# Mixing's steps, priorities, retention and layer-end squares rearranged in a two-layer hybrid trunk

## The chip, the core and the metric

The kernel runs on one core of a Trainium2 chip. The core has TensorE (PE: matmuls, with weight loads shown as PEld), VectorE (DVE), ScalarE (ACT), GpSimd (POOL) and SyncE (SP, which here only issues DMAs). Each takes its instructions in the order in which they were queued at build time, and waits on semaphores for what it needs from the others. The metric is the device time of one execution in microseconds (us), lower is better.

## The reference

The program is a decoder trunk of two layers over 512 tokens of width 1024. Each layer does this (cut to what matters):

```
h = rmsnorm(x, g_mix)
(cq, ckv, kr, aq, ak, av, qi, ki, wi, rq, rk, rv, rg) = split(h @ w_in)
# A) latent attention, 8 heads
q  = rmsnorm(cq) @ w_uq;  kv = rmsnorm(ckv) @ w_ukv
o_a = softmax(causal((q_nope.k_nope + rope(q_rope).rope(kr)) * scale)) @ v
# B) DSA: index scores choose 128 keys per query, 4 heads share one key/value head
score = sum over 8 index heads of wi * relu(rope(qi).rope(ki)), causal
sel = top_k(score, 128);  o_b = softmax over sel of (rope(aq).rope(ak) * scale) @ av
# C) retention, 4 heads: scores times gamma^(i-j), causal, no softmax
ret = (decay * (rope(rq).rope(rk) / 8)) @ rv;  o_c = silu(rg) * groupnorm(ret)
x = x + concat(o_a, o_b, o_c) @ w_out
x = x + square(relu(rmsnorm(x, g_mlp) @ w_ff1)) @ w_ff2
```

After the second layer comes one more rmsnorm.

## The kernel before

Activations lie transposed, features on the 128 partitions and 512 tokens in the free dimension, in tiles of 128x512. Nearly every product is done in reduced-precision F32 (`FR`), with each operand split in a high and a low part: `split` (line 236) copies the high part on ScalarE and forms the remainder on VectorE, `mm3` (148) adds three matmuls. Weights come by DMA from SP's queue and are split the same way (`wsplit`, 203), the remainder on VectorE or GpSimd. A plain F32 matmul, as `pv_step` (335) uses it for MLA's values with a single term, is one call but shows as two matmul instructions in the trace.

A layer has two parts. *Mixing* is a list of steps in the string `ORDER`, read at the end of the layer loop. `qi` are the index queries, `tk` the token-major tiles (`token_tiles`: values of DSA and retention, index weights), `ix` the index scores of one block of 128 queries (ScalarE's relu, VectorE's weighted sum), `rq`/`rk` retention's queries and keys, `rg` its gate, `aq` DSA's queries, `kv`/`cq` the compressed inputs with `kvf`/`cqf` their norms (`LowRank.factor`), `mk`, `k`, `q`, `v`, `rr` MLA's keys, queries, values and rotary parts by pair or round, `m` the maxima of a pair of heads, `a` the attention of one head, `dm` the maxima of DSA, `d` DSA's attention for one query block, and `F` flushes the delayed value products. Two kinds of work are dealt out between them: `tN` takes N steps of top-k from a list of 51 (16 rounds for each of three query blocks, each a MAX8 and a MATCH_REPLACE8 on VectorE at lines 761 and 762, then three masks at line 766), and `rN` takes N of 16 retention scores. A number beyond the list's end does nothing. `dm` needs all three masks.

What the engines do is laid out at build time. The program is traced in the order of the steps; `hp(key)` (line 80) lets the instructions inside it stand `PRI[key]` places further ahead (a negative number: further behind); a planner takes the ready instruction that stands first, engine by engine, by its own estimate of times, and the queues that come out are fixed. Only keys that an `hp` call names act: `w` weights, `e` evacuations of products, `t` top-k, `q`, `qm`, `v`, `k`, `rr`, `pv`, `done`, `ret`, `st` statistics, `tab` tables, `cq`, `dm`, `rg`, `aq`, `rope`.

Retention's value product: `ret_score` forms scores of one key block in PSUM, splits them in high and low tiles, GpSimd multiplies both with a causal mask, and two reduced matmuls with lhsT holding the high and low values of one head give a 128-row result whose halves `ret_done` adds.

The *MLP* part is 32 up-projections and a seven-product (Strassen-like) down-projection (`mlp`, from 424). While its last products run, the next layer's norm begins: `half_squares` (363) squares and adds x for half the columns, `half_stats` (370) reduces the partitions with matmuls by a column of ones, in F32, and `half_bcast` spreads the result. The early half (columns 256 to 511) is done inside the last weight loop, the late half after it.

Of the kernel before, what the change touches and what calls it, by code (L numbers as in the profile page):

```python
# [10 lines left out]
F32 = mybir.dt.float32  # L11
# [6 lines left out]
P = 128  # L18
# [32 lines left out]
OPT_R = 0  # L51
MHI = 'aaap'
MLO = 'vp'
ORDER = 'qi0 rg0 qi1 tk ix1 ix2 F rq0 ix3 rk0 rq1 r1 t2 r1 r1 t3 rk1 t4 rg1 aq1 r1 r1 aq0 F t2 t2 F F F F F t2 F F kv0 kv1 F F t1 F F r2 cq0 t2 t2 r1 r1 cq1 r4 kvf kvc t2 cq2 cq3 t5 r7 cq4 t1 t4 r16 t4 t2 cq5 r12 F F r6 r12 t1 F r2 v0 r16 r14 F r14 r9 cqf r2 t4 mk F t2 r1 r2 cqc r2 r2 r3 F t1 r11 rr0 t1 t4 t4 q0 r4 k1 t5 F k0 t2 r4 F t2 r2 q1 t4 r6 t4 r2 F t10 t10 t3 t4 m0 r2 r6 t2 r5 m1 r3 r2 r1 t3 t2 t5 a0 a1 t2 k2 t4 t4 dm t7 t4 r10 r1 t9 rr1 r1 t7 t3 r2 t4 a2 q2 a3 q3 t3 r3 m2 r7 t6 r10 r2 d2 t5 d3 d0 t15 d1 k3 t4 t2 r2 t2 t1 t3 m3 v1 a4 t8 t1 a6 F t3 r2 t4 t59 t2 r1 t6 r2 a7 r2 t3 t1 t3 a5 t2 t3 F r1 F r3 r2 r10 F r2 F'
PRI = {'fin': 0, 'w': 99, 'e': 59, 't': -225, 'rope': 0, 'split': 133, 'q': -16, 'qm': 0, 'rr': 0, 'v': 5, 'k': 0, 'att': 0, 'pv': 0, 'done': -70, 'ret': -44, 'st': 65, 'x': 0, 'tab': -20, 'cq': 0, 'tok': 15, 'idx': 0, 'dm': 8, 'rg': 0, 'km': 0, 'qi': 0, 'aq': 0}
TOPK = 128
NEG = -1e30
GONE = -3e38
# [10 lines left out]
def trunk_kernel(ctx, tc, xT, gains, win, wtk, wuq, wukv, wout, wff1, wff2, tabs, cf, cb, outT):  # L69
# [20 lines left out]
    def g_(dt=F32, shape=None):  # L90
        return S("g", GB, shape, dt)
# [21 lines left out]
    def p_():  # L113
        return S("p", PB, [P, 2, T], FR)

    def v_(shape, dt=FR):
        return S("v", 2, shape, dt)
# [21 lines left out]
    def R(ap):  # L139
        return ap.bitcast(F32)  # L140

    def tt(eng, op, out, a, b):
        (nc.vector if eng == "v" else nc.gpsimd).tensor_tensor(out, a, b, op=op)
# [92 lines left out]
    def split(src, hi, lo, eng="a"):  # L236
        copy_fr(hi, src, eng)
        nc.vector.tensor_sub(lo, src, R(hi))
# [87 lines left out]
    def push(f):  # L326
        pend.append(f)
        while len(pend) > LAG:
            pend.popleft()()
# [33 lines left out]
    def half_squares(xv, n, cols):  # L363
        t = [g_(F32, [P, 2, 256]) for _ in range(2)]
        for i in range(2):
            nc.scalar.activation(t[i], xv[2 * n + i][:, :, cols], AF.Square)
        nc.vector.tensor_add(t[0], t[0], t[1])
        return t[0]

    def half_stats(sums):  # L370
        with hp("st"):
            ps = sc_ps()
            for n, s in enumerate(sums):
                for m in range(2):
                    for b in range(2):
                        nc.tensor.matmul(ps[:, b : b + 1], s[:, m, b * P : (b + 1) * P], ones,  # L376
                                         start=n + m + b == 0, stop=n + m == 2, skip_group_check=True)
            return rstd(ps[:, :2], 1024)

    def half_bcast(y, ps):  # L380
# [43 lines left out]
    def mlp(l, xv, u, rb, nxt):  # L424
# [172 lines left out]
        for j in range(4, 8):  # L597
            w4[j] = weights(j, "a22", in_qk)
            if j == 5:
                for q in range(4):  # L600
                    for m in range(2):
                        nxt.tile(xv, q, m, early)
                nxt.finish(xv, early, [half_squares(xv, n, early) for n in range(2)])
            if j < 6:
                for n in range(2):
                    mul(p4, w4[j][n], operand(2 * j + n, 1), 2 * j + n)
        sums = []
        for m in range(4):
            for i in range(12, 16):
                mul(p4, w4[i // 2][i % 2], operand(i, 1), i, ms=(m,))  # L610
            with hp("e"):
                o = [xv[m // 2 * 2 + blk][:, m % 2, late] for blk in range(2)]
                nc.vector.tensor_add(o[0], o[0], p4[m][0])
                nc.vector.tensor_sub(o[1], o[1], p4[m][0])
            for blk in range(2):
                nxt.tile(xv, m // 2 * 2 + blk, m % 2, late)
            if m % 2:
                sums.append(half_squares(xv, m // 2, late))
        return sums

    xsrc = xT
    for l in range(DEPTH):
# [79 lines left out]
        wtoks = []  # L702

        def token_tiles():
            vall = v_([P, 4 * T])
            vd = S("vd", 1, [P, NB, 192])
            vr = vall.rearrange("p (b h s d) -> p b h s d", b=NB, h=4, s=2)
            vt.extend((vd, None, vall.rearrange("p (b h d) -> p b h d", b=NB, h=4)))
            for c0 in (0, 128):
                nc.gpsimd.memset(vd[:, :, c0 : c0 + 64], 1.0)  # L710
            wtok = tiny(32, "wtok", 1)
            wtoks.append(wtok)
            tps = [mm_ps(), mm_ps(), o_ps(), o_ps()]
            for c in range(3):
                nk = min(3, KD - 3 * c)
                for j, (h_, l_) in enumerate(wchunk(wtk[l, c][:, : nk * 328], nk * 328, nk)):
                    k = 3 * c + j
                    ah, al = u[k]
                    for b in range(NB):
                        bs = slice(b * P, (b + 1) * P)  # L720
                        mm3(tps[b][:, :328], ah[:, bs], al[:, bs], h_, l_, k == 0, k == KD - 1)
            for b in range(NB):
                o = tps[b]
                z = g_()
                with hp("e"):
                    nc.scalar.activation(z[:, :328], o[:, :328], AF.Copy, scale=rtok[:, b : b + 1])
                nc.vector.tensor_scalar(wtok[:, b * 8 : b * 8 + 8], z[:, 320:328], IDX_SCALE, None, op0=ALU.mult)
                mu = tiny(4)
                zv = z[:, 64:320].rearrange("p (h d) -> p h d", h=4)
                nc.vector.tensor_reduce(mu, zv, axis=AX.X, op=ALU.add)  # L730
                nc.vector.tensor_scalar(mu, mu, 1.0 / 64, None, op0=ALU.mult)
                nc.vector.tensor_sub(zv, zv, mu.rearrange("p (h o) -> p h o", o=1).to_broadcast([P, 4, 64]))
                nc.scalar.activation(vd[:, b, 64:128], z[:, :64], AF.Copy)
                split(zv, vr[:, b, :, 0], vr[:, b, :, 1])

        mix = [(None, None)] * 8
        fill_top, fill_ret = deque(), deque()
# [64 lines left out]
        def ret_score(pr, e, i):  # L802
            (rq, rql), (rk, _) = rqk[3, pr], rqk[5, pr]
            q0 = P * min(i, 2)
            n = T - q0
            ps = sc_ps()[:, :n]
            ks = slice(i * P, (i + 1) * P)
            mm(ps, rk[:, e, ks], rq[:, e, q0:], True, False)
            mm(ps, rk[:, e, ks], rql[:, e, q0:], False, True)
            pt = p_()[:, :, :n]  # L810
            ph, pl = pt[:, 0], pt[:, 1]
            split(ps, ph, pl)
            w = P if i < 3 else 2 * P
            mb = m01[:, 2 * P - w :].rearrange("p (o n) -> p o n", o=1).to_broadcast([P, 2, w])
            tt(E_MSK, ALU.mult, pt[:, :, :w], R(pt[:, :, :w]), mb)
            v = vt[2][:, i, 2 * pr + e]
            push(lambda: pv_step("r", i, [(v, ph), (v, pl)], lambda o: ret_done(pr, e, o)))

        def ret_done(pr, e, o):
            with hp("ret"):  # L820
                rows = slice(64 * e, 64 * e + 64)
                if e == 0:
                    rts[pr] = g_()
                rt = rts[pr]
                half = g_()
                nc.scalar.activation(half[rows], o[64 - 64 * e : 128 - 64 * e], AF.Copy)
                nc.vector.tensor_add(rt[rows], o[rows], half[rows])
                if e == 0:
                    return
                sg = sgs[pr]  # L830
                sq = g_()
                nc.scalar.activation(sq, rt, AF.Square)
                ps = sc_ps()
                mm(ps, blk, sq, True, True)
                yv = g_()
                nc.scalar.activation(yv, ps, AF.Ln, bias=epst)
                nc.scalar.activation(yv, yv, AF.Exp, scale=-0.5)
                nc.gpsimd.tensor_mul(sq, yv, yv)
                nc.vector.scalar_tensor_tensor(sq, ps, EPS, sq, op0=ALU.add, op1=ALU.mult)
                nc.gpsimd.tensor_scalar(sq, sq, -0.5, 1.5, op0=ALU.mult, op1=ALU.add)  # L840
                nc.gpsimd.tensor_mul(yv, yv, sq)
                nc.vector.scalar_tensor_tensor(rt, rt, gcol(G0 + G_RET + pr), yv, op0=ALU.mult, op1=ALU.mult)
                nc.gpsimd.tensor_mul(rt, rt, sg)
                mh, ml = u2()
                split(rt, mh, ml)
                mix[6 + pr] = (mh, ml)
# [513 lines left out]
```

## Time and profile before

| | us |
|---|---|
| median of 3 runs | 1358.52 (1355.89 to 1358.78) |
| the profiled execution, its own time | 1358.57 |
| its span, first to last instruction | 1356.8 |
| TensorE busy | 1298.3 |
| VectorE busy | 1025.6 |
| ScalarE busy | 627.5 |
| GpSimd busy | 272.5 |

A busy TensorE is not one at its peak, because matmuls overlap and their ends are modelled. Layer 0's mixing takes about the first 350 us, its MLP ends near 685 us; layer 1 follows in the same pattern. Line numbers in the rows are those of the kernel before; a line such as 146, 238 or 143 is a helper's, so the names out<-in tell the step.

### The profile page before, as it was taken

The page shows a single profiled execution, that of the slowest core. Times are in us where ns is not written, and L with a number is a line of the kernel's source. Part 1 is how long each engine was busy: PE and PEld are TensorE (multiplying, and loading weights), DVE is VectorE, ACT ScalarE, POOL GpSimd, SP SyncE. Part 2 cuts the span into 40 slices and gives each one's busy share as a digit, 9 for nine tenths or more (in the row PEclk, how much of TensorE's full clock was granted, in tenths as well). Part 3 has the DMA queues.
Part 4 walks back from the last instruction along what each step waited for, and adds up shares of the span by engine and source line. Part 5 has one row for each costly group of instructions (what it writes and reads, how often), then busy time and mean ns, then how long its engine had stood idle before and what let it go on. Part 6 is the DMA issues. An engine that isn't in the chain of part 4 may idle for free. (4 is left out here: it accounts for less than half of the span.)

```text
span 1356.8 us, 19944 instructions
## 1 busy us (share of the span) xinstructions
PE 1298.3 (96%) x7274; PEld 1097.0 (81%) x7276; DVE 1025.6 (76%) x1728; ACT 627.5 (46%) x1083; POOL 272.5 (20%) x265
## 2 busy tenths in 40 slices
PE   9987979999999999999999898899999999999997
PEld 7866866768888888899987677666778888889997
DVE  5799997655777776797668999965558767778875
ACT  4533544654444444465536244446444444445552
POOL 3446752104000000000033467410230000000000
PEclk9989999999999999999999999999999999999998
DMA  6666422223554555466456681232235554554652
GB/s 217 175 179 183 125 73 85 92 63 109 166 176 157 184 186 172 140 209 213 153 163 175 171 206 55 78 114 75 66 109 177 192 175 156 186 184 157 198 184 72
DMA packets 82178, 201.73 MB, mean 149 GB/s; under 512 B 10240, under 2 KB 19168, under 8 KB 82080
## 3 DMA queue, kind: packets, MB, share of 16 engines
q1 hardware_dynamic: 80928, 199.41, 48.0%
q8 instruction: 57, 0.93, 0.3%
q10 hardware_dynamic: 1152, 1.05, 0.2%
q14 instruction: 41, 0.34, 0.1%
HBM read 155.68 MB, written 20.97 MB: 130 GB/s over the span
## 5 line engine op out<-in xcount | busy, mean ns | idle before, releaser
L146 PE MATMUL mm<-u,wh 128*128 128x512 f32 (+1 forms) x1776 | 552.3, 391 | 0.9 <-ACT wh L192 0.9
L146 PEld LDWEIGHTS mm<-u,wh 128*128 128x128 f32 x1776 | 332.1, 190 | 66.5 <-ACT wh L192 1.1
L146 PE MATMUL mm<-u,wl 128*128 128x512 f32 (+1 forms) x888 | 345.6, 389 | 5.7 <-DVE wl L215 5.6
L192 ACT ACTIVATE wh<-wr 128x512 fp32r<-128x512 f32 (+2 forms) x247 | 149.8, 610 | 298.7 <-PE mm L146 187.9
L215 DVE TENSOR_TENSOR wl<-wr,wh 128x512 fp32r<-128x512 f32 (+2 forms) x208 | 148.6, 716 | 85.4 <-ACT wh L192 84.2
L217 POOL TENSOR_TENSOR wl<-wr,wh 128x512 fp32r<-128x512 f32 (+2 forms) x80 | 104.6, 1308 | 487.4 <-ACT wh L192 454.8
L146 PEld LDWEIGHTS mm<-u,wl 128*128 128x128 f32 x888 | 168.3, 190 | 40.7 <-DVE wl L215 7.2
L503 DVE TENSOR_TENSOR u<-wr,u 128x1024 fp32r<-128x1024 f32 x54 | 65.9, 1224 | 25.9 <-ACT u L502 25.8
L502 ACT ACTIVATE u<-wr 128x1024 fp32r<-128x1024 f32 x54 | 57.1, 1058 | 54.3 <-PE o L516 14.1
L445 DVE TENSOR_TENSOR sm<-wr 128x512 f32<-128x512 f32 x64 | 44.2, 691 | 47.8 <-DMA wr<-in_wff 47.8
L516 PEld LDWEIGHTS sc<-g,v 128*128 128x128 f32 x576 | 72.2, 189 | 2.3
L516 PE MATMUL sc<-g,v 128*128 128x256 f32 x576 | 73.1, 281 | 0.0
L433 DVE SCALAR_TENSOR_TENSOR g<-mm,g 128x512 f32<-128x512 f32 x64 | 43.9, 686 | 15.5 <-PE mm L146 15.5
L194 POOL TENSOR_SCALAR wh<-wr 128x512 fp32r<-128x512 f32 (+3 forms) x41 | 30.5, 743 | 107.3 <-PE mm L146 54.1
L762 DVE MATCH_REPLACE8 g<-m,g 128x384 f32<-128x384 f32 (+2 forms) x96 | 51.4, 540 | 0.0
L146 PE MATMUL sc<-u,qk 97*128 97x512 f32 (+5 forms) x192 | 50.0, 384 | 0.9 <-DMA u<-mr 0.9
L516 PE MATMUL o<-g,v 128*128 128x256 f32 x384 | 50.5, 281 | 0.0
L761 DVE MAX8 m<-g 128x8 f32<-128x256 f32 (+2 forms) x96 | 49.9, 546 | 0.1
L449 ACT ACTIVATE v<-wr 128x1024 fp32r<-128x1024 f32 x32 | 34.0, 1062 | 33.2 <-DVE wr L447 33.1
L516 PEld LDWEIGHTS o<-g,v 128*128 128x128 f32 x384 | 47.5, 189 | 0.0
L516 PE MATMUL sc<-wh,u 128*128 128x256 f32 x224 | 46.1, 285 | 0.9 <-ACT wh L486 0.6
L342 PE MATMUL o<-p,v 128*128 128x256 f32 (+2 forms) x128 | 44.8, 462 | 0.5 <-DVE g L1046 0.5
(299 smaller groups left out, 2590.8 us busy)
## 6 DMA issues: line engine op xcount, KB each, us to landing
wr<-in_wff SPq DMA_DIRECT2D x160, 512.0 KB, 3.8
wr<-in_win SPq DMA_DIRECT2D x37, 512.0 KB, 5.7
ws<-sm SPq DMA_DIRECT2D x32, 512.0 KB, 6.0
wr<-ws SPq DMA_DIRECT2D x32, 512.0 KB, 4.4
tab<-in_tabs SPq DMA_DIRECT2D x20, 512.0 KB, 3.9
wr<-in_wout SPq DMA_DIRECT2D x16, 512.0 KB, 5.2
p<-p SPq DMA_DIRECT2D x40, 128.0 KB, 3.0
wr<-in_wuq SPq DMA_DIRECT2D x12, 384.0 KB
```

The costliest lines, as they stand in the source:

```text
L146: return nc.tensor.matmul(out, lhsT, rhs, start=start, stop=stop)
L192: return nc.scalar.activation(out, src, AF.Copy)
L215: order["wl"] = nc.vector.tensor_sub(lo, rc, R(hi))
L217: nc.gpsimd.tensor_sub(lo, rc, R(hi))
L342: nc.tensor.matmul(o[:, q0:], *terms[0], start=i == 0, stop=i == NB - 1, skip_group_check=True)
L433: nc.vector.scalar_tensor_tensor(r, ps, 0.0, rb, op0=ALU.max, op1=ALU.mult)
L445: nc.vector.tensor_add(sm[:, h], w[0], w[1])
L502: nc.scalar.activation(wh, t, AF.Copy)
L503: nc.vector.tensor_sub(wl, t, R(wh))
L516: nc.tensor.matmul(outs[m][0], a[:, m * P : m * P + P], b, start=i == 0 and outs[m][1] and n == 0, stop=i == KP - 1 and n == 2, skip_group ...
L761: nc.vector.max(m8, accs[j])
L762: nc.vector.match_replace(out=accs[j], in_to_replace=m8, in_values=accs[j], imm_value=GONE)
```

## The change

The order of mixing's steps and the priorities are laid out anew; top-k's and retention's steps are dealt out singly, the last two of top-k directly ahead of `dm`, and DSA's blocks stand between steps of MLA's pairs. Retention keeps probabilities and values in F32: one F32 matmul with the values of a pair of heads as lhsT, of whose 128 rows each head uses its 64. At layer ends GpSimd adds planes of squares before the ones-matmuls.

```diff
--- before.py
+++ after.py
@@ -51,8 +51,8 @@
 OPT_R = 0
 MHI = 'aaap'
 MLO = 'vp'
-ORDER = 'qi0 rg0 qi1 tk ix1 ix2 F rq0 ix3 rk0 rq1 r1 t2 r1 r1 t3 rk1 t4 rg1 aq1 r1 r1 aq0 F t2 t2 F F F F F t2 F F kv0 kv1 F F t1 F F r2 cq0 t2 t2 r1 r1 cq1 r4 kvf kvc t2 cq2 cq3 t5 r7 cq4 t1 t4 r16 t4 t2 cq5 r12 F F r6 r12 t1 F r2 v0 r16 r14 F r14 r9 cqf r2 t4 mk F t2 r1 r2 cqc r2 r2 r3 F t1 r11 rr0 t1 t4 t4 q0 r4 k1 t5 F k0 t2 r4 F t2 r2 q1 t4 r6 t4 r2 F t10 t10 t3 t4 m0 r2 r6 t2 r5 m1 r3 r2 r1 t3 t2 t5 a0 a1 t2 k2 t4 t4 dm t7 t4 r10 r1 t9 rr1 r1 t7 t3 r2 t4 a2 q2 a3 q3 t3 r3 m2 r7 t6 r10 r2 d2 t5 d3 d0 t15 d1 k3 t4 t2 r2 t2 t1 t3 m3 v1 a4 t8 t1 a6 F t3 r2 t4 t59 t2 r1 t6 r2 a7 r2 t3 t1 t3 a5 t2 t3 F r1 F r3 r2 r10 F r2 F'
-PRI = {'fin': 0, 'w': 99, 'e': 59, 't': -225, 'rope': 0, 'split': 133, 'q': -16, 'qm': 0, 'rr': 0, 'v': 5, 'k': 0, 'att': 0, 'pv': 0, 'done': -70, 'ret': -44, 'st': 65, 'x': 0, 'tab': -20, 'cq': 0, 'tok': 15, 'idx': 0, 'dm': 8, 'rg': 0, 'km': 0, 'qi': 0, 'aq': 0}
+ORDER = 'qi0 tk rg0 qi1 ix1 ix3 F ix2 F t1 rk0 rq0 rq1 rk1 r1 t1 r1 F t1 r1 t1 r1 F t1 t1 t1 t1 t1 t1 t1 t1 t1 F t1 aq1 t1 aq0 r1 F r1 t1 rg1 kv0 kv1 r1 t1 F r1 t1 t1 t1 cq0 F t1 F r1 r1 cq1 r1 t1 t1 r1 r1 t1 kvf r1 t1 t1 kvc t1 F cq2 cq3 t1 F t1 t1 t1 t1 cq4 r1 t1 t1 t1 r1 t1 t1 t1 t1 t1 t1 v0 cq5 t1 F cqf t1 t1 mk rr0 t1 F t1 F k1 F t1 F q0 t1 k0 F q1 F m0 m1 t1 a0 a1 t1 t1 dm rr1 q2 a2 k2 a3 d1 q3 k3 F F d3 m3 d2 F d0 m2 v1 a6 a7 a4 a5 F F'
+PRI = {'fin': 90, 'w': 99, 'e': 11, 't': -122, 'rope': 0, 'split': 168, 'q': -16, 'qm': 155, 'rr': 0, 'v': 125, 'k': 0, 'att': 135, 'pv': 0, 'done': -65, 'ret': -39, 'st': -25, 'x': 85, 'tab': -50, 'cq': 160, 'tok': 116, 'idx': 72, 'dm': 21, 'rg': -12, 'km': -174, 'qi': -41, 'aq': -7}
 TOPK = 128
 NEG = -1e30
 GONE = -3e38
@@ -371,10 +371,9 @@
         with hp("st"):
             ps = sc_ps()
             for n, s in enumerate(sums):
-                for m in range(2):
-                    for b in range(2):
-                        nc.tensor.matmul(ps[:, b : b + 1], s[:, m, b * P : (b + 1) * P], ones,
-                                         start=n + m + b == 0, stop=n + m == 2, skip_group_check=True)
+                for b in range(2):
+                    nc.tensor.matmul(ps[:, b : b + 1], s[:, b * P : (b + 1) * P], ones,
+                                     start=n + b == 0, stop=n == len(sums) - 1, skip_group_check=True)
             return rstd(ps[:, :2], 1024)
 
     def half_bcast(y, ps):
@@ -600,7 +599,10 @@
                 for q in range(4):
                     for m in range(2):
                         nxt.tile(xv, q, m, early)
-                nxt.finish(xv, early, [half_squares(xv, n, early) for n in range(2)])
+                t = [half_squares(xv, n, early) for n in range(2)]
+                nc.gpsimd.tensor_add(t[0], t[0], t[1])
+                nc.gpsimd.tensor_add(t[0][:, 0], t[0][:, 0], t[0][:, 1])
+                nxt.finish(xv, early, [t[0][:, 0]])
             if j < 6:
                 for n in range(2):
                     mul(p4, w4[j][n], operand(2 * j + n, 1), 2 * j + n)
@@ -615,7 +617,10 @@
             for blk in range(2):
                 nxt.tile(xv, m // 2 * 2 + blk, m % 2, late)
             if m % 2:
-                sums.append(half_squares(xv, m // 2, late))
+                t = half_squares(xv, m // 2, late)
+                if m == 1:
+                    nc.gpsimd.tensor_add(t[:, 0], t[:, 0], t[:, 1])
+                sums.extend(t[:, n] for n in range(1 if m == 1 else 2))
         return sums
 
     xsrc = xT
@@ -702,10 +707,9 @@
         wtoks = []
 
         def token_tiles():
-            vall = v_([P, 4 * T])
+            vall = v_([P, NB, 4, 64], F32)
             vd = S("vd", 1, [P, NB, 192])
-            vr = vall.rearrange("p (b h s d) -> p b h s d", b=NB, h=4, s=2)
-            vt.extend((vd, None, vall.rearrange("p (b h d) -> p b h d", b=NB, h=4)))
+            vt.extend((vd, None, vall.rearrange("p b (r e) d -> p b r (e d)", r=2)))
             for c0 in (0, 128):
                 nc.gpsimd.memset(vd[:, :, c0 : c0 + 64], 1.0)
             wtok = tiny(32, "wtok", 1)
@@ -729,9 +733,8 @@
                 zv = z[:, 64:320].rearrange("p (h d) -> p h d", h=4)
                 nc.vector.tensor_reduce(mu, zv, axis=AX.X, op=ALU.add)
                 nc.vector.tensor_scalar(mu, mu, 1.0 / 64, None, op0=ALU.mult)
-                nc.vector.tensor_sub(zv, zv, mu.rearrange("p (h o) -> p h o", o=1).to_broadcast([P, 4, 64]))
+                nc.vector.tensor_sub(vall[:, b], zv, mu.rearrange("p (h o) -> p h o", o=1).to_broadcast([P, 4, 64]))
                 nc.scalar.activation(vd[:, b, 64:128], z[:, :64], AF.Copy)
-                split(zv, vr[:, b, :, 0], vr[:, b, :, 1])
 
         mix = [(None, None)] * 8
         fill_top, fill_ret = deque(), deque()
@@ -807,14 +810,12 @@
             ks = slice(i * P, (i + 1) * P)
             mm(ps, rk[:, e, ks], rq[:, e, q0:], True, False)
             mm(ps, rk[:, e, ks], rql[:, e, q0:], False, True)
-            pt = p_()[:, :, :n]
-            ph, pl = pt[:, 0], pt[:, 1]
-            split(ps, ph, pl)
+            p = pf_()[:, :n]
+            nc.scalar.activation(p, ps, AF.Copy)
             w = P if i < 3 else 2 * P
-            mb = m01[:, 2 * P - w :].rearrange("p (o n) -> p o n", o=1).to_broadcast([P, 2, w])
-            tt(E_MSK, ALU.mult, pt[:, :, :w], R(pt[:, :, :w]), mb)
-            v = vt[2][:, i, 2 * pr + e]
-            push(lambda: pv_step("r", i, [(v, ph), (v, pl)], lambda o: ret_done(pr, e, o)))
+            tt(E_MSK, ALU.mult, p[:, :w], p[:, :w], m01[:, 2 * P - w :])
+            v = vt[2][:, i, pr]
+            push(lambda: pv_step("r", i, [(v, p)], lambda o: ret_done(pr, e, o)))
 
         def ret_done(pr, e, o):
             with hp("ret"):
@@ -822,9 +823,7 @@
                 if e == 0:
                     rts[pr] = g_()
                 rt = rts[pr]
-                half = g_()
-                nc.scalar.activation(half[rows], o[64 - 64 * e : 128 - 64 * e], AF.Copy)
-                nc.vector.tensor_add(rt[rows], o[rows], half[rows])
+                nc.scalar.activation(rt[rows], o[rows], AF.Copy)
                 if e == 0:
                     return
                 sg = sgs[pr]
```

## Rows read from the trace of the kernel before

**Rows 1.** The page, part 1: busy us, share of the span, instructions of each engine.
```profile
PE 1298.3 (96%) x7274; PEld 1097.0 (81%) x7276; DVE 1025.6 (76%) x1728; ACT 627.5 (46%) x1083; POOL 272.5 (20%) x265
```

**Rows 2.** Stretch, its length, busy PE, PEld, DVE, ACT, POOL; then PEclk, DMA share, GB/s.
```profile
50.00:215.00 165.00, 144.58 (x640) 114.25 (x640) 156.48 (x317) 72.79 (x149) 91.48 (x85) 0.95 0.50 138
215.00:350.00 135.00, 132.59 (x645) 97.14 (x645) 78.91 (x116) 68.95 (x129) 28.19 (x28) 1.00 0.29 88
350.00:575.00 225.00, 225.00 (x1240) 196.49 (x1239) 169.46 (x273) 97.17 (x153) 0.00 (x0) 1.00 0.54 173
740.00:885.00 145.00, 127.73 (x576) 100.78 (x574) 136.30 (x280) 60.47 (x118) 78.90 (x78) 0.95 0.49 132
```

**Rows 3.** TensorE's timeline (start, us, instruction, count): reduced-precision products, then F32 ones.
```profile
157.24 0.40 PE L146 MATMUL o<-p,v 128*128 128x256 f32 x2
157.48 0.28 PE L146 MATMUL sc<-qk,qk 128*128 128x256 f32 x1
...
165.71 0.61 PE L146 MATMUL mm<-u,wh 128*128 128x512 f32 x2
166.16 0.39 PE L146 MATMUL mm<-u,wl 128*128 128x512 f32 x1
...
219.56 1.02 PE L342 MATMUL o<-p,v 128*128 128x512 f32 x2
220.02 0.91 PE L146 MATMUL sc<-u,qk 128*128 128x384 f32 x2
220.77 0.23 PE L146 MATMUL sc<-cbt 128*128 128x128 bf16 x1
```

**Rows 4.** VectorE's groups in layer 0's mixing: count | busy us, mean ns | idle before.
```profile
L761 DVE MAX8 m<-g 128x8 f32<-128x512 f32 x16 | 10.9, 680 | 0.0
L762 DVE MATCH_REPLACE8 g<-m,g 128x512 f32<-128x512 f32 x16 | 10.8, 674 | 0.0
...
L238 DVE TENSOR_TENSOR p<-sc,p 128x256 fp32r<-128x256 f32 x8 | 3.1, 412 | 0.0
L827 DVE TENSOR_TENSOR g<-o,g 64x512 f32<-64x512 f32 x4 | 2.7, 684 | 0.2 <-ACT g L826 0.2
L238 DVE TENSOR_TENSOR p<-sc,p 128x512 fp32r<-128x512 f32 x4 | 2.7, 677 | 0.0
...
L238 DVE TENSOR_TENSOR v<-g,v 128x256 fp32r<-128x256 f32 x4 | 2.6, 660 | 0.0
...
L238 DVE TENSOR_TENSOR p<-sc,p 128x384 fp32r<-128x384 f32 x4 | 2.2, 546 | 0.0
```

**Rows 5.** GpSimd's groups from 50 to 215 us: the causal masks.
```profile
L143 POOL TENSOR_TENSOR p<-p,cft 128x256 fp32r<-128x256 f32 x12 | 10.3, 870 | 12.8 <-DVE p L238 12.0 <-DVE tiny L243 0.7
...
L143 POOL TENSOR_TENSOR p<-p,cft 128x512 fp32r<-128x512 f32 x4 | 5.6, 1408 | 2.5 <-DVE p L238 2.5
```

**Rows 6.** TensorE's timeline: ones-matmuls of the early half at layer 0's end.
```profile
667.13 1.02 PE L376 MATMUL sc<-ones,g 128*128 128x1 f32 x8 [0.21 <-DVE g L367]
...
668.58 0.95 PE L376 MATMUL sc<-ones,g 128*128 128x1 f32 x8
```

**Rows 7.** Line 143 (tt) of VectorE: shortest, median and longest ns.
```profile
L143 DVE TENSOR_TENSOR p<-p,tab x22: 668/692/1781, 29.7 to 892.2; 128x512 f32<-128x512 f32 x22
```

**Rows 8.** TensorE's waits in the whole span: us in total, times, longest.
```profile
PE sc L271 <- DVE tiny L908: 4.7, 4, 1.4
```

**Rows 9.** Waits in SP's queue in the whole span.
```profile
SPq L308 <- DVE p L671: 36.4, 4, 11.2
```

**Rows 10.** Timeline: the last top-k mask and the first DSA maximum, layers 0 and 1.
```profile
204.22 1.23 DVE L766 TENSOR_SCALAR ma<-g 128x512 bf16<-128x512 f32 x1
...
223.35 0.47 PE L146 MATMUL sc<-km,qk 128*128 128x256 f32 x1
...
881.33 0.43 DVE L766 TENSOR_SCALAR ma<-g 128x512 bf16<-128x512 f32 x1
...
886.87 0.47 PE L146 MATMUL sc<-km,qk 128*128 128x256 f32 x1
```

## The prediction, made before the changed kernel was run

> **What bounds the kernel now.** I read the page's busy shares first, then busy time by stretch, then waits inside the slow stretches. TensorE is busy 96% of the span [rows 1], which looks like a closed case; the table by stretch opens it [rows 2]. In the MLP (350 to 575 us) TensorE is busy without a break. In the second half of mixing (215 to 350) it is idle 2.4 us of 135. Nearly all the idle time lies in the first half of mixing: 165 - 144.6 = 20.4 us in layer 0 (50 to 215) and 145 - 127.7 = 17.3 us in layer 1 (740 to 885), 37.7 us together, and the granted clock averages 0.95 there (some windows at the 1.2 GHz level), 1.00 elsewhere. In exactly these two stretches VectorE is busy 156.5 of 165 us (95%) and 136.3 of 145 us (94%); after them it drops to 58%. So mixing has two regimes: first VectorE sets the pace (index sums, 48 top-k rounds, ropes, weight remainders, retention), then TensorE does. The border is the last top-k mask, whose end lets the DSA maxima begin.
>
> Beside this row stands a rule of the Trainium skill, Perfetto Trace Analysis, Optimization Strategy: where the most-contended engine changes over time, interleaving the regimes may help. It is what the new step order would have to achieve; the trace shows the two regimes, no run yet shows what mixing them returns.
>
> **The change part by part.** *Retention in F32, TensorE's side.* A head now takes two matmuls in reduced-precision F32 (p's high and low part) for each of four key blocks of 512, 384, 256 and 256 columns; after, one full F32 matmul, which the chip runs as two passes, as MLA's values do already. From the starts of matmuls [rows 3]: two reduced ones of 512 begin 0.45 us apart from the next, so 0.225 each; two of 256 take 0.24, so 0.12; 384 between them, 0.17. A head costs 2 x (0.225 + 0.17 + 0.12 + 0.12) = 1.27 us. For F32, from 219.56 to 220.77 us TensorE does two passes of 512 and two reduced matmuls of 384: 1.21 - 0.34 = 0.87 us. Scaled by columns: 0.87 + 0.65 + 0.43 + 0.43 = 2.38 us a head. The change adds 1.1 us a head, with 4 heads in 2 layers **+8.9 us of TensorE work**.
>
> *Its VectorE side* [rows 4]. Gone in a layer: the remainders of 16 score tiles, 8 x 0.412 + 4 x 0.677 + 4 x 0.546 = 8.2 us; the 4 remainders of the values, 2.6 us; the 4 sums of the two halves, 2.7 us (the copy that ScalarE made for them now writes the result). That is 13.5 us a layer, **27 us in all**, and all of it lies in the VectorE-bound stretches, ahead of the last mask. GpSimd's causal mask halves in width: 12 x 0.87 + 4 x 1.41 = 16.1 us a layer [rows 5] becomes about 8, and no longer waits for a remainder. ScalarE's work stays, less four small copies.
>
> What is this worth? If VectorE's time alone set the end of those stretches, all 27 us; TensorE's idle 37.7 us would fall to 37.7 - 27 - 8.9 = 2 us, which would need TensorE saturated, though there are waits in those stretches that a lighter VectorE doesn't end (a sum of squares, a transposed factor, a DMA). If VectorE's work was only filler around such chains, nothing. I take the middle, **-13 us**, with the F32 passes covered: TensorE then still idles 16 us there. If that cover is gone, they cost their 8.9 us.
>
> *Squares added by GpSimd.* The early half of a layer end now reduces its four 256-column planes to one before the ones-matmul: 16 instructions become 4; the late half, 16 become 12. Eight take 0.95 us, 0.12 each [rows 6]; 24 early ones make 2.9 us in a saturated stretch. The late 8 count little: after the last VectorE sum there are eight as before. Against it stand GpSimd's adds of 128x512 and 128x256; the nearest row of that engine is the 1.41 us for 512 columns [rows 5], so some 2.1 us on the early chain, beside which TensorE still has second-product matmuls. Bounds: -3.5 if hidden, +1 if TensorE waits 2.1 us at both early ends. I take **-2.5 us**, nearer the hidden end since TensorE waited 0.21 us for that chain at 667 us [rows 6].
>
> A rule of the Trainium skill speaks against these adds: SBUF — State Buffer, Who interferes with whom, says a VectorE instruction with two SBUF inputs and a GpSimd instruction that reads SBUF exclude each other for the whole instruction. The trace agrees so far: VectorE's rope multiply has a median of 0.69 us and a longest of 1.78 [rows 7], while GpSimd works on the same ropes. By it the adds could hold VectorE's remainders at a layer end for up to 2.8 us, and the halved masks would give back up to 8 us a layer; the sum goes without either.
>
> *Order and priorities.* Only keys that the code asks for act: top-k rises from -225 to -122, so its rounds are less pure filler, and their steps now stand one by one, the last two directly ahead of the DSA maxima; statistics fall from 65 to -25, evacuations from 59 to 11, tables from -20 to -50; the compressed queries, values and MLA maxima rise (160, 125, 155). Index scores move ahead of all retention products, so top-k can begin sooner. One gain I can name: the factor's transposes, placed with high priority, hold TensorE until VectorE's small chain is done, 4.7 us in four places [rows 8]; at -25 other products may go first. I take **-4 us**. Moved retention products bring a table load, 2 swaps and 8 or 4 row copies each to SP, in whose queue the swaps waited 36.4 us in four places for an evacuation [rows 9], with weight loads behind them; evacuations at 11 and tables at -50 could make that longer. DSA between MLA pairs falls in a stretch with 2.4 us idle, so it is worth 0 to 2 us. Bounds for order: -16 (the idle that is left above) to +16 (below).
>
> **Sum.** The profiled execution took 1358.6 us (span 1356.8 and 1.8 around it), the same as the median of 1358.5. 1358.6 - 13 - 2.5 - 4 = **1339 us**.
>
> **The rivals.** *A: the cover was real and all comes back.* VectorE's 27 us, squares 3.5, order 8: 1320 us. For: 95% busy with 8.5 us idle in 165. Against: TensorE would need to be saturated.
>
> *B: the new places eat the gain.* Half of retention's 13 us is lost again to evacuations that come later or tables that land later, and the statistics gain nothing: 1358.6 - 6 - 2 + 4 = 1355 us, between 1350 and 1361. For: many moves, each in-order queue is rearranged. Against: VectorE is really lighter.
>
> *C: TensorE's passes decide.* The stretches are set by chains through TensorE, the remainders were filler, and F32 is paid: 1358.6 + 8.9 - 2.5 = 1365 us. It decides once a retention head finds TensorE without idle time beside it. For: TensorE is the engine with 96%. Against: the idle time is in this very stretch.
>
> *D, the other side: top-k comes too late for the DSA maxima.* Now the last mask is done at 204.22 + 1.23 = 205.45 us and the maxima begin at 223.35, 17.9 us of slack; in layer 1 it is 881.33 + 0.43 = 881.8 and 886.87, only 5.1 [rows 10]. A round with 512 columns takes 0.68 + 0.67 us [rows 4]. If seven of the 48 rounds (about 8 us) still stand in line when TensorE comes to the maxima, it waits 8 us a layer, and the stretch keeps its old length: 1358.6 + 16 - 2.5 = 1372 us. It decides once top-k ends later than the other work ahead of the maxima. For: the last two steps stand right ahead of them. Against: higher priority, an earlier start, 13.5 us less for VectorE.
>
> **How the numbers follow.** Forecast (1330 to 1350 us) 0.49, A 0.17, B 0.15, C 0.11, D 0.08. The range, 1320 to 1366 us, leaves out the better half of A (0.08), a little of C and all of D, about 0.19. The likeliest case's own range is 1330 to 1350. A measurement of this kernel can tell 0.2% (2.7 us) from no change: faster than 1355.8 is the forecast, A and half of B, 0.74; slower than 1361.2 is C and D, 0.19; between them 0.07.
>
> **What would show it.** Right: the stretch from 50 us to the last top-k mask shorter by 5 to 13 us in each layer, VectorE about 13 us less busy in mixing, TensorE's idle there under 15 us a layer, its clock nearer 1.00; second half of mixing and MLP unchanged within 2 us. The retention values as 32 F32 matmuls (64 passes) of 0.43 us per 512 columns; 32 instead of 64 ones-matmuls at the layer ends. Wrong: stretches as long as before with VectorE idle in them (C); TensorE waiting at the DSA maxima for a mask (D); waits on SP's swaps or on tables grown past 10 us (B).

## The result and the profile after

The changed kernel took 1338.5 us (median of four executions; 1337.7 without the one left out below) against 1358.5, ratio 0.9847 with a 95% interval of 0.9816 to 0.9879: 1.5% faster, where 1339 us had been forecast. Timed again beside the other kernels of the study (e1) it took 1336.0, ratio 0.9828 (0.9803 to 0.9853). One execution of the first timing, its profiled one (2118 us at a mean granted clock of 0.555), one of e3 (3261 us) and one of e8 (4439 us) are left out, and the profile below is that of e1 (1336.4 us, span 1334.7).

Differences in us below are ratios to the kernel before on the same chip, times 1358.5 us, with 0.9828 for the changed kernel. e1 to e4 were timed on one chip, e5 to e12 on another. There the changed kernel itself was not timed, but e10, whose engines execute the same instructions in the same order, gave 0.9809. So a difference of 2.6 us between two kernels says nothing, and beside e10 each of the losses in e5 to e12 would be 2.6 us larger.

Busy time in the whole span, then by stretch (length, PE, PEld, DVE, ACT, POOL, clock, DMA share, GB/s), after:

```profile
PE 1294.6 (97%) x7242; PEld 1091.0 (82%) x7244; DVE 998.1 (75%) x1680; ACT 622.5 (47%) x1075; POOL 262.2 (20%) x271
```

```profile
50.00:215.00 165.00, 152.47 (x683) 117.78 (x682) 141.70 (x289) 73.81 (x148) 85.05 (x88) 0.98 0.55 153
731.00:876.00 145.00, 132.77 (x595) 102.00 (x593) 124.78 (x260) 61.67 (x122) 76.20 (x82) 0.96 0.50 136
350.00:575.00 225.00, 225.00 (x1285) 198.44 (x1285) 169.87 (x272) 101.27 (x158) 0.00 (x0) 1.00 0.53 173
```

Beside [rows 1, 2]: VectorE does 27.5 us less (1025.6 to 998.1), as forecast, and is busy 86% of both early stretches instead of 95 and 94%. TensorE idles 12.5 and 12.2 us there instead of 20.4 and 17.3, although it now does the F32 passes; 350 to 575 us is as busy as before. The layer-1 stretch is shifted by 9 us, about what layer 0 has gained. In the whole span TensorE was idle 1356.8 - 1298.3 = 58.5 us and is idle 1334.7 - 1294.6 = 40.1: of the 22.1 us that the span lost, 18.4 were idle time of TensorE.

The granted clock, a mean over times at the 2.4 and the 1.2 GHz level, rose with it: from 0.95 to 0.98 and from 0.95 to 0.96 in the two stretches, and from 0.985 to 0.991 as the mean of whole runs beside e1. Among the 29 runs of the kernel before on that chip, a run is shorter by 1.1 us for each 0.001 that its clock is higher. By this estimate some 7 of the 23 us go along with the clock; whether the clock gives them or only follows TensorE's shorter idle time, no run shows.

The parts of the change are in the trace. Groups of TensorE and GpSimd (count | busy us, mean ns | idle before), after:

```profile
L342 PE MATMUL o<-p,v 128*128 128x512 f32 x48 | 24.9, 601 | 0.7 <-POOL p L143 0.6
...
L375 PE MATMUL sc<-ones,g 128*128 128x1 f32 x32 | 4.2, 238 | 1.8 <-DVE g L367 0.9 <-POOL g L622 0.9
```

```profile
L143 POOL TENSOR_TENSOR p<-p,cft 128x128 f32<-128x128 f32 x12 | 6.2, 524 | 8.9 <-ACT p L814 6.7 <-DMA wr<-in_wukv 2.1
...
L143 POOL TENSOR_TENSOR p<-p,cft 128x256 f32<-128x256 f32 x4 | 2.9, 735 | 0.0
```

F32 value products with 512 columns are now 48 passes, MLA's 32 and retention's 16; the ones-matmuls at layer ends fell from 64 to 32. The masks cost 9.1 us a layer instead of 15.9 [rows 5].

The border of the two regimes is where the prediction goes astray. The last top-k mask and the first DSA maximum in the timeline, after, layers 0 and 1:

```profile
172.43 1.44 DVE L769 TENSOR_SCALAR ma<-g 128x512 bf16<-128x512 f32 x1
...
215.32 0.28 PE L146 MATMUL sc<-km,qk 128*128 128x256 f32 x1
...
830.38 2.02 DVE L769 TENSOR_SCALAR ma<-g 128x512 bf16<-128x512 f32 x2
...
873.66 0.28 PE L146 MATMUL sc<-km,qk 128*128 128x256 f32 x1
```

Beside [rows 10]: the masks are done 32 and 49 us earlier (5 to 13 had been forecast), the maxima begin only 8.0 and 13.2 us earlier. 41 us lie between them in either layer, so top-k does not set when the maxima begin. (The maxima of the first query block add a constant mask, `cq256`, so top-k's masks are needed later still.)

Where the 22.1 us of span went, by the maxima's starts: before the first of them 8.0 (223.35 to 215.32); from there to layer 1's 5.2 (663.5 to 658.3); from there to the end 8.9 (469.9 to 461.0). The last is not early mixing. From the maxima to the last residual add of mixing layer 1 took 117.8 us (the add starts at 1004.71) and takes 112.0 (985.64); layer 0 took 114.3 (337.60) and takes 112.0 (327.33). The stretch of layer 1 before and after, in the columns of [rows 2]:

```profile
886.90:1004.70 117.80, 115.84 (x557) 84.14 (x557) 70.95 (x100) 59.42 (x111) 26.34 (x25) 1.00 0.28 86
```

```profile
873.70:985.60 111.90, 111.59 (x546) 81.89 (x546) 70.78 (x99) 58.46 (x110) 24.61 (x23) 1.00 0.27 81
```

Not all of these 5.8 us are saved. TensorE has 11 matmul instructions fewer there, 212,352 columns instead of 219,264; at the prediction's 0.225 us for 512 columns that is 3.0 us of work that now stands ahead of the maxima or behind the add. Its idle time fell by 1.7 us (117.80 - 115.84 to 111.90 - 111.59).

### The profile page after: what moved, and what is told of

Same layout as the page of the kernel before. It is cut to its first block, busy times and chain, and to the rows that moved or that the text cites. A ratio compares the mean times of both kernels' runs of the same rounds, so it can differ in the third digit from the quotient of the medians.

```text
span 2116.5 us, 19831 instructions
## 1 busy us (share of the span) xinstructions
PE 2105.8 (99%) x7244; PEld 1457.7 (69%) x7244; DVE 998.2 (47%) x1680; ACT 629.1 (30%) x1075; POOL 252.1 (12%) x271
## 4 chain that ended last, share of the span: by engine, by line
PE 99%; issue 0%; DVE 0%; ACT 0%; POOL 0%; DVEq 0%; POOLq 0%
PE mm L146 58%; PE sc L515 12%; PE sc L146 8%; PE o L515 6%; PE mm L515 6%; PE o L342 5%; PE o L146 3%; PE sc L647 1%; PE sc L159 0%; PE sc L271 0%; PE sc L375 0%; DVE g L419 0%; PE sc L381 0%; PE sc L1027 0%; POOL p L143 0%
## 5 line engine op out<-in xcount | busy, mean ns | idle before, releaser
L146 PE MATMUL mm<-u,wh 128*128 128x512 f32 (+1 forms) x1776 | 848.3, 572 | 0.0
L146 PEld LDWEIGHTS mm<-u,wh 128*128 128x128 f32 x1776 | 392.5, 225 | 263.6 <-issue 156.8
L146 PE MATMUL mm<-u,wl 128*128 128x512 f32 (+1 forms) x888 | 505.4, 572 | 0.0
L192 ACT ACTIVATE wh<-wr 128x512 fp32r<-128x512 f32 (+3 forms) x247 | 150.5, 610 | 832.9 <-PE mm L146 747.5
L217 POOL TENSOR_TENSOR wl<-wr,wh 128x512 fp32r<-128x512 f32 (+3 forms) x80 | 97.5, 1218 | 335.2 <-ACT wh L192 298.1
L515 PEld LDWEIGHTS sc<-g,v 128*128 128x128 f32 x576 | 114.3, 265 | 10.1 <-issue 4.7
L515 PE MATMUL sc<-g,v 128*128 128x256 f32 x576 | 117.3, 383 | 0.0
L342 PE MATMUL o<-p,v 128*128 128x512 f32 (+1 forms) x192 | 115.5, 723 | 0.7 <-POOL p L143 0.7
L146 PE MATMUL mm<-qk,wh 128*128 128x512 f32 x128 | 61.4, 576 | 0.0
L515 PEld LDWEIGHTS sc<-wh,u 128*128 128x128 f32 x224 | 57.6, 296 | 0.0
L515 PE MATMUL sc<-v,u 128*128 128x256 f32 x264 | 56.9, 380 | 0.0
```

The source lines that it names most:

```text
L146: return nc.tensor.matmul(out, lhsT, rhs, start=start, stop=stop)
L192: return nc.scalar.activation(out, src, AF.Copy)
L217: nc.gpsimd.tensor_sub(lo, rc, R(hi))
L342: nc.tensor.matmul(o[:, q0:], *terms[0], start=i == 0, stop=i == NB - 1, skip_group_check=True)
L515: nc.tensor.matmul(outs[m][0], a[:, m * P : m * P + P], b, start=i == 0 and outs[m][1] and n == 0, stop=i == KP - 1 and n == 2, skip_group ...
```

## The experiments

Each is one change against the kernel before or against the changed one; the rest of its text is theirs.

**e1**: the changed kernel again. 

> The changed kernel again, for a profile at the usual clock. Theory (VectorE's lighter load shortens the first half of mixing, which VectorE sets): about 1338 us; the stretch up to the last top-k mask shorter by 5 to 13 us in each layer, TensorE idle there under 15 us a layer, second half of mixing and MLP unchanged within 2 us. Rival (the new places of the steps alone make the gain): VectorE as busy a share of the stretch as before, and the gain in waits of TensorE for chains, in either half of mixing.

Measured: 1336.0 us. VectorE's share fell, TensorE's idle time is under 15 us a layer; but the second half of mixing became shorter too, by 2.3 and 5.8 us, where the theory had it unchanged within 2 us.

**e2**: the kernel before with F32 retention alone.

```diff
-            split(ps, ph, pl)
+            nc.scalar.activation(p, ps, AF.Copy)
...
-            push(lambda: pv_step("r", i, [(v, ph), (v, pl)], lambda o: ret_done(pr, e, o)))
+            push(lambda: pv_step("r", i, [(v, p)], lambda o: ret_done(pr, e, o)))
```

> The kernel before with retention in F32 alone; order, priorities and squares as before. Theory: 13 us of VectorE's 27 come through and the F32 passes are covered: about 1346 us (1340 to 1352). Rival, order alone: VectorE's rounds of top-k only fill, TensorE pays its passes: 1358 to 1367 us.

Measured: 1360.7 us, ratio 1.0032 (1.0007 to 1.0057): no gain, some 4 us lost (by the interval 1 to 8). VectorE's stretch row and the timeline of e2 say why (it has the old order):

```profile
50.00:215.00 165.00, 145.94 (x637) 114.81 (x636) 146.05 (x294) 70.73 (x144) 83.96 (x85) 0.95 0.51 138
```

```profile
174.04 0.68 DVE L764 TENSOR_SCALAR ma<-g 128x384 bf16<-128x384 f32 x2
...
223.93 0.47 PE L146 MATMUL sc<-km,qk 128*128 128x256 f32 x1
```

VectorE is 10 us freer than in [rows 2], and its last masks are done by 174.7 us instead of 205.4. The maxima begin at 223.93, half a microsecond later than in [rows 10]. In layer 1 the last mask is done 39 us earlier (843.0) and the maxima begin 3.8 us later (890.7). The lighter engine only finished its filler earlier. My theory falls for the old order.

**e3**: the kernel before with the new `ORDER` and `PRI` alone. 

> The kernel before with the new order and priorities alone. Theory: order is worth some 4 us: about 1354 us (1350 to 1358). Rival, order alone: 1335 to 1343 us, nearly the whole gain.

Measured: 1349.9 us, ratio 0.9933 (0.991 to 0.9957), 9 us faster: more than the theory's 4, less than half of the whole. Of its 10.1 us of span (maxima at 221.87 and 883.28 us, end at 1346.7) 6.5 lie behind layer 1's maxima and only 1.5 ahead of layer 0's. The last masks are done at 217.4 and 882.8 us: late, but still 4.5 and 0.5 us ahead of the maxima.

**e4**: the kernel before with GpSimd's squares alone.

```diff
+                nc.gpsimd.tensor_add(t[0], t[0], t[1])
+                nc.gpsimd.tensor_add(t[0][:, 0], t[0][:, 0], t[0][:, 1])
+                nxt.finish(xv, early, [t[0][:, 0]])
```

> The kernel before with the layer-end squares added by GpSimd alone. Theory: 32 instructions of 0.12 us go, GpSimd's adds are hidden: about 1356 us (1355 to 1357.5). Rival: TensorE waits for GpSimd at the early halves: 1358.5 to 1361 us.

Measured: 1359.3 us, ratio 1.001 (0.9986 to 1.0033), no difference that can be told. TensorE's timeline at layer 0's end in e4:

```profile
669.24 0.60 PE L375 MATMUL sc<-ones,g 128*128 128x1 f32 x4 [1.27 <-POOL g L604]
```

Four instructions take 0.60 us where 16 took 1.97 [rows 6], but they wait 1.27 us for GpSimd where 0.21 had been waited: the wait takes most of what the fewer matmuls save.

**e5**: the changed kernel with retention split as before (e2's edit undone). 

> The changed kernel with retention split as before (new order, priorities and squares stay). Theory now (retention's relief of VectorE pays only in the new order, where top-k ends just ahead of the DSA maxima): 1347 to 1351 us, so retention is worth 11 to 15 us there, against nothing in the old order. Rival (the parts simply add, and the rest of the gain is from squares): 1336 to 1341 us.

Measured: 1351.6 us, ratio 0.9943 (0.9907 to 0.998). So on the new layout F32 retention is worth 1.2%, 15.6 us, where it lost 4 on the old. TensorE's matmuls with retention's masked scores, and what they wait for (us, times, longest): before, e3, e5, and the changed kernel:

```profile
PE o L146 <- POOL p L143: 1.5, 1, 1.5
```

```profile
PE o L146 <- POOL p L143: 11.6, 10, 2.3
```

```profile
PE o L146 <- POOL p L143: 12.0, 11, 2.1
```

```profile
PE o L342 <- POOL p L143: 4.4, 5, 2.4
```

With split retention the new layout makes TensorE wait some 12 us for GpSimd's masked scores; in the old layout it waited 1.5. F32 retention takes 7.6 us of that away. (Weight loads, which overlap the matmuls, show the same wait as 2.8, 17.4, 18.8 and 7.5 us.) A second wait stands behind it in retention's chain, for the squares of its group norm (`ret_done`), in e5 and in the changed kernel:

```profile
PE sc L146 <- ACT g L837: 7.2, 3, 3.4
```

```profile
PE sc L146 <- ACT g L831: 2.0, 1, 2.0
```

F32 retention has no sum of two halves ahead of these squares; 5.2 us less are waited. The two together are 12.8 us.

The chain is the link that I had missed. From the end of ScalarE's copy of a score to the end of its mask it takes 5.1 us on average before, 3.3 in e5 and 1.1 in the changed kernel. So the old layout, with the longest chain, hardly waits for it: it leaves room for it, and the new one does not. Of the 3.3 us in e5, 1.25 pass until VectorE's remainder is done, 1.0 until GpSimd begins and 1.0 in the mask.

VectorE's queue also stands in the chain of work that ended last (as the profile infers it from semaphores; shares of the whole span). On the page of e3, which has split retention and the new layout, and on that of the changed kernel, where the chain can be followed back to 155 us:

```profile
PE 79%; DVE 12%; issue 3%; ACT 2%; DMA 2%; POOL 2%; DVEq 0%; ACTq 0%; POOLq 0%
```

```profile
PE 77%; DVE 5%; DMA 2%; issue 2%; ACT 1%; POOL 1%; SPq 0%; DVEq 0%; POOLq 0%; ACTq 0%
```

Of layer 1's early mixing alone VectorE holds 43% in e3 (740 to 883 us), 46% in e5 (764 to 887) and 11% in the changed kernel (740 to 873); top-k's rounds hold 16, 17.5 and 2.4%. So with split retention on the new layout VectorE's full queue is on the path after all, though not by top-k's masks: in e5 those are done 4.5 and 0.7 us ahead of the maxima (216.4 and 886.6 us). The next runs change parts of it.

**e6**: the changed kernel plus VectorE's remainders, their result unused.

```diff
             nc.scalar.activation(p, ps, AF.Copy)
+            nc.vector.tensor_sub(S("dum", 1)[:, :n], ps, p)
```

> The changed kernel with F32 retention, plus the 16 VectorE remainders a layer put back with their result unused (8.2 us a layer); TensorE's and GpSimd's work is that of the changed kernel. Theory: VectorE's time is what the relief was worth: 1343 to 1348 us, some two thirds of the loss without F32 retention. Rival (the gain of F32 retention is the shorter chain from score to product and GpSimd's halved mask): 1336 to 1339 us.

Measured: 1341.4 us, ratio 0.9862 (0.9831 to 0.9893), 4.6 us slower than the changed kernel, their intervals overlapping: less than the two thirds expected, if anything. But e6 does not add load alone. The mask overwrites the tile that the remainder reads, so GpSimd has to wait for VectorE again, as long in all as in e5 (22.2 us there):

```profile
POOL p L143 <- DVE dum L815: 22.4, 17, 3.9
```

TensorE's wait for masked scores rises from 4.4 to 7.5 us. So 4.6 us is the price of load and link together.

**e7**: the changed kernel with one reduced matmul for each value product.

```diff
-            p = pf_()[:, :n]
+            p = pf_()[:, :n].bitcast(FR)
...
-            vall = v_([P, NB, 4, 64], F32)
+            vall = v_([P, NB, 4, 64])
```

> The changed kernel with retention's probabilities and values rounded to one reduced-precision part each, so one reduced matmul instead of F32's two passes; the low parts are left out of the product. TensorE's work falls by 2.38 - 0.63 = 1.75 us a head, 14 us in all; other engines' work stays. Theory (the passes are covered by TensorE's idle time): 1331 to 1336 us. Rival (TensorE's work is on the path): 1322 to 1327 us.

Measured: 1333.0 us, ratio 0.9807 (0.9772 to 0.9843): 3 us back of 14, hardly more than two timings of the same order differ (e10). The F32 passes are covered for the most part, as the prediction had it.

**e8**: the changed kernel with the old `ORDER`. 

> The changed kernel with the old step order; new priorities, F32 retention and squares stay. If priorities carry the layout's gain (statistics later, compressed queries and maxima earlier): 1336 to 1343 us. If the step order carries it (index scores ahead of retention, retention's and top-k's steps dealt out singly): 1350 to 1360 us.

Measured: 1354.8 us, ratio 0.9959 (0.9937 to 0.998). The priorities alone don't carry the gain. Still it is some 10 us faster than e2, which has the same order and F32 retention with the old priorities.

**e9**: the changed kernel with every mask of retention done twice by GpSimd.

```diff
+            tt(E_MSK, ALU.mult, S("dum", 1)[:, :w], p[:, :w], m01[:, 2 * P - w :])
             tt(E_MSK, ALU.mult, p[:, :w], p[:, :w], m01[:, 2 * P - w :])
```

> The changed kernel with GpSimd's causal mask of retention done twice (once into an unused tile), some 8 us more of GpSimd a layer, as much as the split form had. If the mask's width carries part of what the remainders (5 us) did not: 1340 to 1345 us. If GpSimd is off the path: 1335 to 1338 us.

Measured: 1348.9 us, ratio 0.9919 (0.9892 to 0.9947), 12.4 us slower than the changed kernel. TensorE's wait for masked scores in e9:

```profile
PE o L342 <- POOL p L143: 10.9, 13, 3.2
```

It rises from 4.4 to 10.9 us, by 6.5 (on weight loads from 7.5 to 19.9). The added masks as GpSimd's groups in e9, 50 to 215 us:

```profile
L143 POOL TENSOR_TENSOR dum<-p,cft 128x128 f32<-128x128 f32 x12 | 6.5, 538 | 8.8 <-ACT p L814 8.5 <-DVE m L764 0.3
...
L143 POOL TENSOR_TENSOR dum<-p,cft 128x256 f32<-128x256 f32 x4 | 3.1, 763 | 0.0
```

9.6 us of an engine that is busy a fifth of the time cost 6.2 us a layer. Instruction by instruction (name and shape, in order of start) e9's queues are nearly those of the changed kernel: moving 38 of TensorE's 7242 and 38 of VectorE's 1680 makes them the same. So this is the cost of a longer mask in the chain score, copy, mask, product, with what the clock adds (mean 0.988 against 0.991 in e1; 0.993 in e6). The chain's length alone does not give the price: from copy to mask's end it is 2.3 us on average in e9 and 2.6 in e6, which lost less.

**e10**: the changed kernel with whole slots for the scores.

```diff
-            p = pf_()[:, :n]
+            p = S("p", PB, [P, 2, T])[:, 0, :n]
```

> The changed kernel with each F32 score tile of retention in a whole slot of the pool p, as the split form had, instead of two tiles a slot. If the slots carry part of the gain: 1340 to 1345 us, with ropes and scores starting later. If not: 1335 to 1338 us.

Measured: 1335.7 us, ratio 0.9809 (0.9777 to 0.984). No effect; the order of instructions on all four engines came out the same, so it also shows how well a time repeats: within 2.6 us of e1.

**e11**: the changed kernel with the old `PRI`. 

> The changed kernel with the old priorities; new step order, F32 retention and squares stay. With the old order and the new priorities it took 1354.8 us. If the order string alone carries the layout: 1337 to 1343 us. If the two only work together: 1348 to 1360 us, the second half of mixing and the first MLP product as long as before (some 2 to 3 us a layer).

Measured: 1367.9 us, ratio 1.005 (1.0024 to 1.0076): slower than the kernel before and than either expectation. The second half of mixing stayed short (maxima at 222.0 and 899.0 us, last residual adds at 333.9 and 1010.7: 111.8 and 111.7 us), so that belongs to the order; the first halves lose more than all: layer 0's maxima come 6.7 us later than in the changed kernel, and layer 1's 18.7 us more after that. It isn't the masked scores: TensorE waits 4.9 us for them, much as in the changed kernel (4.4). What it is stays open.

**e12**: the changed kernel with statistics at 65.

```diff
-'st': -25
+'st': 65
```

> The changed kernel with the statistics at their old priority of 65. Theory (the prediction's one named gain of the layout, 4 us from transposes and sums no longer placed ahead of products): 1339 to 1342 us, with TensorE waiting again for the factor's chain and for GpSimd's sum of squares at the start of the MLP. Rival (other places gained it): 1335 to 1338 us.

Measured: 1351.7 us, ratio 0.9932 (0.9905 to 0.9959), 14 us slower, far more than the 4 expected. It is the named wait only in small part: TensorE waits 4.6 us for the factor's chain (3.4 in the changed kernel). Its wait for masked scores rose from 4.4 to 10.4 us and that for GpSimd's squares at the layer ends from 0.9 to 5.0. To make the two orders the same, 201 of TensorE's 7242 instructions have to be moved. One number of the priorities, moving 3% of the instructions, costs more than half of the gain.

## Why the prediction was right, and where it was not

The time was right within 3 us, and the cover of the F32 passes was right on the new layout (e7). The sum's terms were not what they were taken for, and that the total came out is in part luck: tried apart on the kernel before, retention, order and squares gave +4, -9 and nothing, -5 us together. The other 18 us come from their interaction, for which the sum has no term.

*Retention, -13 us.* The size came out (15.6 us on the new layout), the reason only in part. Two steps failed. "The border is the last top-k mask": e2 moves that mask 31 us and the maxima not at all. "VectorE sets the pace": on the old layout a 95% busy engine was filling gaps with top-k, and its relief is worth nothing (e2). On the new layout with split retention VectorE's queue is on the path (e5), but what TensorE waits for at the end of it are retention's masked scores and the squares of its group norm: 19.2 us, and 6.4 with F32 retention. What the prediction left without a value, GpSimd's halved mask, which "no longer waits for a remainder", carries a large part: doubling the mask costs 12.4 us (e9), the remainders, which the mask then waits for again, 4.6 (e6). That the two, 17 us, come near the 15.6 is no proof: both lengthen one chain, and at e1's clock, by the estimate above, they would be some 9 and 6 us. How the gain divides between the mask's width, the remainder ahead of it, the sum of the halves and VectorE's plain load stays open.

*Order, -4 us.* Mis-sized, and not a term by itself. Alone, order and priorities give 9 us, mostly behind the maxima, where I had expected no more than 2: layer 1's second half fell by 5.8 us and layer 0's by 2.3, partly by work that now stands elsewhere, and with the old priorities (e11) they are as short. In the first half their gain was lost again to some 17 us of new waits (e3: 11.6 us for masked scores instead of 1.5, 6.6 for the group norm's squares instead of none), until F32 retention took most of these away. That is the interaction: -9 and +4 apart, -23.4 together. Nor do order and priorities add: on the old order the new priorities are worth some 10 us (e8 against e2), on the new one 30 (the changed kernel against e11), all with F32 retention.

*Squares, -2.5 us.* Not confirmed. The instructions went, but TensorE waited for GpSimd instead (e4), near the outer bound of that term; with the new layout no difference shows either (e5 against e3).

*Rivals.* A, that all of VectorE's time comes back, fell with e2. C, that the passes decide, came true in part on the old layout, where e2 lost some 4 us. D did not come: 41 us of slack, though only 0.5 with split retention (e3, layer 1). B, that the new places eat the gain, is what e3 shows for its first half, with another culprit than the tables and evacuations that I named.

The rule of the Trainium skill, Perfetto Trace Analysis, Optimization Strategy, that interleaving regimes may help agrees with the trace as to the goal (VectorE at 86% in the early stretches, TensorE less idle); that interleaving did it, no run shows by itself. For the rule of the Trainium skill, SBUF — State Buffer, Who interferes with whom, no run here changes one thing alone: in e9 GpSimd's double work left VectorE's rope multiply at a median of 0.69 us and a longest of 1.79, as in [rows 7], and VectorE's busy time in all rose by 3.3 us (998.1 to 1001.4).

Open: which moves in the two strings matter, and what the clock's share is. The ablations e5, e8, e11 and e12 also lay the queues anew, so a few us in them may belong to the layout and not to the part taken out; only e9 and e10 are nearly free of that. No run disturbed the layout with the work unchanged.

## What to carry to other kernels

A busy engine is a bound only if the work at its end is waited for: look at how long its last product lies before its use (here 18 us, then 41) before pricing its relief, and look again once the layout is another one (0.5 us in e3). Price a chain across engines by the consumer's wait, link by link, small links too: some 0.5 to 0.8 us more of mask for each score cost 12.4 us in all. An added instruction whose result nobody uses can still delay whoever overwrites its input (e6). With queues laid out by a planner, parts don't add: a layout and the work that it was fitted to have to be measured together.

## What the runs showed of the hardware

GpSimd's causal mask takes 0.52 us for 128 F32 columns against 0.87 for the reduced-precision pair of 2 x 128 [rows 5]: 0.60 of the time for half the width; for 256 against the pair of 2 x 256 it is 0.74 against 1.41 us, 0.52 of the time. Four F32 ones-matmuls behind a wait (e4, 0.60 us) show how little a count of small TensorE instructions says beside one wait of 1.27 us.
